# Split FFN weights kept in device memory by pass one and fetched by passes two and three; both variances ahead of the finishing steps

## The chip, the cores and the metric

The kernel runs on one core of a Trainium2 chip. The core has five engines that run their own instruction streams side by side and wait for each other through semaphores: TensorE (matmuls; PE in the profile, with its weight loads as PEld), VectorE (DVE), ScalarE (ACT), GpSimd (POOL) and SyncE (SP). Here SP does nothing but issue transfers; 16 DMA engines carry them between device memory and the core's on-chip memory. Matmul results land in PSUM, eight banks of 128 x 512 float32. The metric is the device time of one execution in microseconds; lower is better.

## What is computed

One layer of a streaming encoder over 2048 tokens of width 1024. First a token mixer (spatial gating) beside a cross-attention into 256 memory tokens, an output projection, a residual and a layer norm. Then a SwiGLU feed-forward network (FFN) of width 2816, a residual and a second layer norm. The change touches the FFN and its norms:

```python
def layer_norm(x, g, b):
    xf = x.astype(jnp.float32)
    mu = jnp.mean(xf, -1, keepdims=True)
    var = jnp.mean(jnp.square(xf - mu), -1, keepdims=True)
    y = (xf - mu) * lax.rsqrt(var + LN_EPS)
    return (y * g.astype(jnp.float32) + b.astype(jnp.float32)).astype(x.dtype)

def swiglu_ffn(x, w_in, w_down):
    h = x @ w_in
    return (jax.nn.silu(h[..., :D_FF]) * h[..., D_FF:]) @ w_down
...
        x = layer_norm(DEEPNORM_ALPHA * x + branch @ w_o[i], ln1_g[i], ln1_b[i])
        x = layer_norm(DEEPNORM_ALPHA * x + swiglu_ffn(x, ffn_w_in[i], ffn_w_down[i]), ln2_g[i], ln2_b[i])
```

## The kernel before

Everything is laid out feature-major: features on the 128 partitions, tokens along the free axis. Every operand of a matmul is split in two parts, `hi` (rounded to the float32r format) and `lo` (the rest), and a product is three matmuls: hi x hi, hi x lo, lo x hi (`PASSES`, L95). The splitting is `split` (L71): ScalarE casts (L73), VectorE subtracts (L74). Activations are split once; weights are split each time that they are loaded.

The mixer part handles the tokens in four chunks of 512 and ends near 752 us of the profile. It writes its normed output to a tensor `x1d` in device memory. The norm of its last chunk runs beside the FFN's start.

The FFN part goes over the tokens in three passes of 688, 680 and 680 tokens (`FPASSES`; here called passes 0, 1 and 2), and each pass goes over all the weights: 22 tiles of the FFN width in blocks of 5, 4, 4, 4 and 5 (`FBLOCKS`). A block has two parts.

- **Up** (`Pass.up`, L345), for each of the block's tiles: the gate and value columns of that tile together, by Strassen's scheme in Winograd's form, over halves of the model width and halves of the tokens. That is seven products of 4 x 3 = 12 matmuls each, every one with its own weight matrix of 128 x 512. `halves` (L97) loads the two weight tiles (r_u, 512 KB each) and makes four sums and differences of them (s_u, L109 to L113), on GpSimd for the first block of a pass and on VectorE for the others. `products` (L115) splits the seven matrices into tiles w, one behind the other, and runs the matmuls. Behind each product VectorE or ScalarE takes a stage (L354 to L368) that adds up the results and ends in silu(gate) x value, which is split into g.
- **Down** (`Pass.down`, L387), for each of the eight output feature tiles: the block's rows of the down projection come from device memory (r_d), are split into w_d (`weights`, L79; one tile for four rows, two tiles of two and three rows for five), and 3 matmuls per row and half of the tokens follow. VectorE adds the result to fa, which starts as the residual that `residual` (L380) loads from x1d (L406 for the first block, L409 for the others).

During the last down block of passes 0 and 1, `load` and `rest` (L319, L335) fetch and split the activations of the next pass. The layer norm of a pass (two `Norm`s, one for each half of its tokens, and one for the mixer's last chunk in pass 0) is taken in small steps between the products of the next pass's first block. `norm_steps` (L257) is a generator: `up` takes one step of it behind each product, 35 in the first block, and what is left is run at the block's end. A norm has these steps: the mean (a matmul with ones) and the centring (`centre`, L184; 4 steps), the variance and its inverse root (`var`, L220, on VectorE, ending in dg), and `finish` (L238; 4 steps), whose first act is a matmul that spreads dg over the partitions (`spread`). Finished tiles are stored to the output; the residual of the pass takes the same memory, so it loads behind those stores.

Three pools of on-chip tiles matter: `raw` (L68), four tiles of 4 KB per partition for anything loaded from device memory; `wsp` (L76), five tiles of 4 KB for split weights; and the eight PSUM banks, of which a tile's products use four. TensorE runs its instructions in the order in which the program emits them (`in_order`, L51). On the other engines, a scheduler chooses the order at build time by its own estimate; each engine then runs its stream strictly in that order. All loads and stores of the FFN part are issued by SP.

Of the kernel before, what the change touches and what calls it, by code (L numbers as in the profile page):

```python
# [17 lines left out]
P = 128  # L18
D = 1024
# [7 lines left out]
KD = D // P            # 8 contraction tiles of the model width  # L27
KB = (MIX + HEADS * HD) // P   # 10 contraction tiles of the branch width
NF = DFF // P          # 22 tiles of the FFN width
TC = 512               # tokens in a chunk of the mixer part  # L30
OPERANDS = (25, 3)             # operand tiles of the up projection that find room before and behind the mixer's end
NCHUNK = SEQ // TC
FPASSES = (688, 680, 680)      # tokens in a pass of the FFN part
# [6 lines left out]
def trunk_kernel(ctx, tc, xT, memT, wv, wuq, ws, bs, vg, vb, wmk, wmv, wo,  # L40
# [10 lines left out]
    def in_order(ins):  # L51
        """TensorE runs its instructions in the order in which they are emitted."""
        if last_on_pe:
            tc.add_manual_dep(ins.ins, last_on_pe.pop().name,
                              mybir.DependencyInfo(mybir.DependencyClass.NoSync, mybir.DependencyReason.DATA),
                              reason="order of TensorE")
        last_on_pe.append(ins.ins)
# [13 lines left out]
    def split(hi, lo, src, engine=nc.vector):  # L71
        """src = hi + lo exactly, each with the bits that one pass of TensorE carries."""
# [6 lines left out]
    def weights(src, shape, name, loads=1):  # L79
        """src [P, *shape], loaded at once and split; as shape[0] pairs [P, 2, shape[1]], several to a tile."""  # L80
        k, r, pairs = shape[0], raw([P, *shape], f"r_{name}"), []
        for i in range(loads):
            s = slice(i * k // loads, (i + 1) * k // loads)
            nc.sync.dma_start(out=r[:, s], in_=src[:, s])
        parts = -(-k * shape[1] // 512)
        for i in range(parts):
            s = slice(i * k // parts, (i + 1) * k // parts)
            n = s.stop - s.start
            w = wsp([P, 2, n, shape[1]], f"w_{name}_{i}")
            split(w[:, 0], w[:, 1], r[:, s])  # L90
# [6 lines left out]
    def halves(wa, wb, name, engine, in_place):  # L97
        """Two output tiles' weights, loaded: the left operands of the seven products in Strassen's scheme (in
        Winograd's form), over the two tiles x the halves of the contraction; by product."""
# [15 lines left out]
    def products(left, right, banks, name, stages, order, s4_after):  # L115
        """The seven products, into four banks; `stages` has the sums behind each of them."""
        q0, q1, q2, q3 = banks
        src, s4 = left
        out = {1: (q0, True, False), 2: (q0, False, True), 3: (q2, False, True), 4: (q3, False, True),
               5: (q2, True, False), 6: (q1, True, True), 7: (q3, True, False)}  # L120
        for n, p in enumerate(order):
            if n == s4_after:
                s4()
            to, start, stop = out[p]
            w = wsp([P, 2, 4, P], f"w{p}_{name}")
            split(w[:, 0], w[:, 1], src[p])
# [17 lines left out]
    def two_tiles(t, m, t0, n):  # L144
        """Feature tiles m and m + 1 of the tokens t0 to t0 + n."""
# [5 lines left out]
    class Norm:  # L151
        """Takes y feature tile by feature tile. Its sums over the tiles run on GpSimd; or, to end soon, on TensorE
        behind a VectorE that takes two tiles at a time (`pairs`)."""
# [24 lines left out]
        def variances(self, sq, start, stop):  # L178
            """One accumulation group for all columns: its start opens the whole bank."""
# [77 lines left out]
    def norm_steps(norms, stores, wait, pad):  # L257
        """The norms in small steps, to be taken between other work."""
# [10 lines left out]
        for _ in range(pad):  # L269
            yield  # L270
        for x, store in zip(norms, stores):
            x.var()
            for _ in range(5):
                yield
            yield from pairs(lambda a, b: x.finish(store, a, b))

    def inv_sqrt(r, v, t):
        """r = v ** -0.5 on VectorE: Newton steps from an estimate made of the bits, half the exponent; t is scratch."""
# [631 lines left out]
```

## Time and profile before

| | us |
|---|---|
| three runs | 2202.60, 2203.41, 2201.05 |
| their median | 2202.6 |
| span of the profiled execution, first to last instruction | 2205.3 |
| FFN part in that execution, first product to the end | 752.1 to 2205.3 |
| pass 0, pass 1, pass 2 begin at | 752.1, 1227.0, 1707.7 |

How to read the views that follow. The page gives busy time by engine; a busy TensorE is not yet one at its pace, since matmuls are pipelined. A row of the view of stretches has: from and to, the length, then for each engine its busy time and the number of its instructions, the TensorE clock that was granted (1.00 is full), the mean busy share of the DMA engines and the rate that they moved. Asked for one tile, such as h (the up projection's results in PSUM) or d (the down projection's), the row counts only the instructions that write or read that tile. A row of waits has: who waited, for whom, the total, the number of times and the longest. A row of groups has: line, engine, operation, out<-in and the count, then busy time and the mean duration in ns of one, then the idle time ahead of the group and what ended it. A row of the timeline has: start, length, engine, line, operation, and in brackets the idle time before it and what ended that. A row of transfers has: what was moved, the queue, the count, the size of one, and the median time from issue to landing.

### The profile page before, as it was taken

The page shows a single profiled execution, that of the slowest core. Times are in us where ns is not written, and L with a number is a line of the kernel's source. Part 1 is how long each engine was busy: PE and PEld are TensorE (multiplying, and loading weights), DVE is VectorE, ACT ScalarE, POOL GpSimd, SP SyncE. Part 2 cuts the span into 40 slices and gives each one's busy share as a digit, 9 for nine tenths or more (in the row PEclk, how much of TensorE's full clock was granted, in tenths as well). Part 3 has the DMA queues.
Part 4 walks back from the last instruction along what each step waited for, and adds up shares of the span by engine and source line. Part 5 has one row for each costly group of instructions (what it writes and reads, how often), then busy time and mean ns, then how long its engine had stood idle before and what let it go on. Part 6 is the DMA issues. An engine that isn't in the chain of part 4 may idle for free.

```text
span 2205.3 us, 34595 instructions
## 1 busy us (share of the span) xinstructions
PE 2120.0 (96%) x13130; PEld 2009.0 (91%) x13130; DVE 1704.4 (77%) x3014; ACT 970.7 (44%) x1886; POOL 397.3 (18%) x294
## 2 busy tenths in 40 slices
PE   9899999999999999999999889999999899999996
PEld 7888798798788889999999889999998899999996
DVE  7986796797788785776778986676689877677677
ACT  5553653654465452433434453343344534334344
POOL 1412321331322440000001820000004700000003
PEclk9999999999999999999999999999999999999998
DMA  6233324234334443212223242222224242221223
GB/s 211 77 110 123 112 78 158 92 96 149 117 96 133 139 132 92 87 58 86 87 68 91 89 160 88 82 68 82 82 66 119 83 153 67 87 86 58 89 75 99
DMA packets 88965, 221.93 MB, mean 101 GB/s; under 512 B 8416, under 2 KB 18656, under 8 KB 88800
## 3 DMA queue, kind: packets, MB, share of 16 engines
q1 hardware_dynamic: 88320, 218.66, 31.9%
q8 instruction: 103, 1.69, 0.3%
q0 software_dynamic: 480, 1.07, 0.2%
q14 instruction: 62, 0.51, 0.1%
HBM read 202.92 MB, written 16.78 MB: 100 GB/s over the span
## 4 chain that ended last, share of the span: by engine, by line
PE 66%; DVE 19%; DMA 5%; issue 4%; ACT 4%; POOL 2%; ACTq 0%; DVEq 0%; POOLq 0%; SPq 0%
PE h L60 36%; PE d L60 19%; PE v L60 5%; PE u L60 3%; DMA r_x<-in_xT 2%; DVE w L74 2%; DVE x L74 2%; DVE w_o L74 1%; DMA r_f<-x1d 1%; DVE w_u L74 1%; PE y L60 1%; POOL s_a L197 1%; ACT p L569 1%; DVE z L526 1%; DVE w_d L74 1%
## 5 line engine op out<-in xcount | busy, mean ns | idle before, releaser
L60 PE MATMUL h<-x,w 128*128 128x340 f32 (+1 forms) x5544 | 886.5, 322 | 14.7 <-DVE w L74 6.5
L60 PEld LDWEIGHTS h<-x,w 128*128 128x128 f32 x5544 | 875.1, 190 | 22.3 <-DVE w L74 8.9
L60 PE MATMUL d<-g,w_d 128*128 128x340 f32 (+3 forms) x3168 | 504.4, 320 | 7.5 <-DVE w_d L74 6.6
L60 PEld LDWEIGHTS d<-g,w_d 128*128 128x128 f32 x3168 | 497.4, 189 | 11.6 <-DVE w_d L74 8.3
L73 ACT CAST w<-s_u 128x512 fp32r<-128x512 f32 x264 | 163.4, 620 | 227.2 <-PE d L60 106.5
L74 DVE TENSOR_TENSOR w<-s_u,w 128x512 fp32r<-128x512 f32 x264 | 195.2, 741 | 46.1 <-ACT w L73 39.1
L60 PE MATMUL y<-br,w_o 128*128 128x512 f32 x960 | 224.4, 395 | 0.0
L60 PEld LDWEIGHTS y<-br,w_o 128*128 128x128 f32 x960 | 180.5, 188 | 42.0
L73 ACT CAST w<-r_u 128x512 fp32r<-128x512 f32 x198 | 122.3, 618 | 166.6 <-PE h L60 67.7
L60 PE MATMUL v<-w_v,x 128*128 128x512 f32 x768 | 188.4, 402 | 6.7 <-ACT w_v L73 5.0
L74 DVE TENSOR_TENSOR w<-r_u,w 128x512 fp32r<-128x512 f32 x198 | 150.0, 759 | 53.0 <-ACT w L73 49.7
L73 ACT CAST w_d<-r_d 128x512 fp32r<-128x512 f32 (+2 forms) x184 | 95.7, 521 | 206.6 <-PE d L60 151.3
L60 PEld LDWEIGHTS v<-w_v,x 128*128 128x128 f32 x768 | 144.1, 191 | 42.1 <-ACT w_v L73 5.0
L409 DVE TENSOR_TENSOR fa<-fa,d 128x340 f32<-128x340 f32 (+3 forms) x192 | 97.2, 506 | 100.3 <-PE d L60 100.3
L330 POOL TENSOR_TENSOR t<-r_f,r_f 128x340 f32<-128x340 f32 (+1 forms) x12 | 14.9, 1244 | 791.1 <-DMA r_f<-x1d 397.4
L74 DVE TENSOR_TENSOR w_d<-r_d,w_d 128x512 fp32r<-128x512 f32 (+2 forms) x184 | 110.5, 603 | 50.3 <-ACT w_d L73 47.1
L73 ACT CAST g<-c 128x340 fp32r<-128x340 f32 (+1 forms) x132 | 63.1, 478 | 93.9 <-DVE c L354 93.9
L60 PE MATMUL u<-xt,w_u 128*128 128x256 f32 x768 | 95.6, 280 | 0.0
L60 PEld LDWEIGHTS u<-xt,w_u 128*128 128x128 f32 x768 | 92.7, 188 | 0.0
L60 PE MATMUL u<-x,w_u 128*128 128x256 f32 x576 | 78.6, 288 | 11.3 <-DVE u L535 6.9
L60 PEld LDWEIGHTS u<-x,w_u 128*128 128x128 f32 x576 | 72.1, 191 | 13.9 <-issue 6.6
L74 DVE TENSOR_TENSOR w_o<-r_o,w_o 128x512 fp32r<-128x512 f32 (+1 forms) x96 | 67.8, 716 | 21.1 <-ACT w_o L73 20.8
(185 smaller groups left out, 2537.6 us busy)
## 6 DMA issues: line engine op xcount, KB each, us to landing
r_u<-in_w SPq DMA_DIRECT2D x132, 512.0 KB, 3.4
r_d<-in_w SPq DMA_DIRECT2D x72, 256.0 KB, 2.7
r_d<-in_w SPq DMA_DIRECT2D x56, 320.0 KB, 2.9
r_u<-in_wuq SPq DMA_DIRECT2D x32, 512.0 KB, 3.6
r_o<-in_wo SPq DMA_DIRECT2D x32, 512.0 KB, 3.6
r_v<-in_wv SPq DMA_DIRECT2D x31, 512.0 KB, 4.4
y<-in_xT SPq DMA_DIRECT2D x16, 512.0 KB, 5.8
x1d<-y SPq DMA_DIRECT2D x16, 512.0 KB, 4.0
```

Of the source, the lines that this page charges most:

```text
L60: in_order(nc.tensor.matmul(*args, **kw))
L73: nc.scalar.copy(hi, src)
L74: engine.tensor_sub(lo, src, hi.bitcast(F32))
L197: nc.gpsimd.tensor_add(self.s2, self.s2, sq)
L330: nc.gpsimd.tensor_sub(t3, b22, b12)
L409: nc.vector.tensor_add(y, y, p)
L526: nc.vector.tensor_scalar(z[h][:, b], z[h][:, b], mv[:, b, 0:1], rs[:, b:b + 1], ALU.subtract, ALU.mult)
L569: nc.scalar.activation(pr[:, h, :], svs[h // 2][:, h % 2, :], AF.Exp, scale=HD ** -0.5, bias=mxv[:, h:h + 1], accum_out=sm[:, h:h + 1])
```

## The change

The first pass splits the weights as before, and then stores each split tile (hi and lo together) to a tensor of its own in device memory. The store is issued from ScalarE's queue (`keep`). Passes 1 and 2 make no weight sums and no splits: they fetch the kept tiles (`ready`), by SP, in turn into a tile of `wsp` and into a tile of `raw`, and the matmuls read those directly. This holds for the up projection's 154 matrices and the down projection's 56 tiles. A fetched tile of the up projection has 512 KB; the two raw tiles that stood for seven matrices had 1 MB together.

In `norm_steps` the order of a seam's steps changes. Before, each norm had its variance, five steps of other work, and its four finishing steps, one norm behind the other. Now both variances come first, with four steps behind each, then four more steps, and then the finishing steps of both. The norms of passes 0 and 1 start after 6 steps instead of 4.

```diff
+    kept = {}
+
+    def keep(key, w):
+        t = dram.tile(list(w.shape), F32, tag=key, name=f"k_{key}")
+        nc.scalar.dma_start(out=t, in_=w.bitcast(F32))
+        kept[key] = t
+
+    turns = []
+
+    def ready(key, name):
+        src = kept[key]
+        turns.append(key)
+        if len(turns) % 2:
+            w = wsp(list(src.shape), f"w_{name}")
+            nc.sync.dma_start(out=w.bitcast(F32), in_=src)
+            return w
+        r = raw(list(src.shape), f"r_{name}")
+        nc.sync.dma_start(out=r, in_=src)
+        return r.bitcast(F32R)
...
     def weights(...):
+        have = key is not None and f"{key}_0" in kept
+        if not have:
+            r = raw([P, *shape], f"r_{name}")
...
+            if have:
+                w = ready(f"{key}_{i}", f"{name}_{i}")
+            else:
+                w = wsp([P, 2, n, shape[1]], f"w_{name}_{i}")
+                split(w[:, 0], w[:, 1], r[:, s])
+                if key is not None:
+                    keep(f"{key}_{i}", w)
...
     def products(...):
-            w = wsp([P, 2, 4, P], f"w{p}_{name}")
-            split(w[:, 0], w[:, 1], src[p])
+            if src:
+                w = wsp([P, 2, 4, P], f"w{p}_{name}")
+                split(w[:, 0], w[:, 1], src[p])
+                if key is not None:
+                    keep(f"{key}_{p}", w)
+            else:
+                w = ready(f"{key}_{p}", f"{p}_{name}")
...
     def norm_steps(norms, stores, wait, pad):
...
+        for x in norms:
+            x.var()
+            for _ in range(4):
+                yield
+        for _ in range(4):
+            yield
         for x, store in zip(norms, stores):
-            x.var()
-            for _ in range(5):
-                yield
             yield from pairs(lambda a, b: x.finish(store, a, b))
...
-            products(halves(w1[f], w1[NF + f], f"u{name}", sums, False), lambda p, k, b: self.x[p][k][:, b], banks,
-                     name, {p: then(stage) for p, stage in stages.items()}, (1, 6, 2, 5, 7, 3, 4), 0)
+            left = None if no else halves(w1[f], w1[NF + f], f"u{name}", sums, False)
+            products(left, lambda p, k, b: self.x[p][k][:, b], banks,
+                     name, {p: then(stage) for p, stage in stages.items()}, (1, 6, 2, 5, 7, 3, 4), 0, key=f"u{f}")
...
-                return weights(w2[m, :, f0:f0 + nb, :], [nb, P], f"d{no}_{blk}_{m}_{ci}")
+                return weights(w2[m, :, f0:f0 + nb, :], [nb, P], f"d{no}_{blk}_{m}_{ci}", key=f"d{blk}_{m}")
...
-                work = norm_steps(norms, [pa.store(0, h), pa.store(h, n)], 4, 0)
+                work = norm_steps(norms, [pa.store(0, h), pa.store(h, n)], 6, 0)
```

More of the change, by code (lines that the diff above doesn't have):

```diff
@@ L77, in wsp, with weights @@
         return common.tile(shape, F32R, tag="wsp", bufs=5, name=name)
[L79 to L84, printed above, removed]
-        parts = -(-k * shape[1] // 512)
-        for i in range(parts):
-            s = slice(i * k // parts, (i + 1) * k // parts)
-            n = s.stop - s.start
-            w = wsp([P, 2, n, shape[1]], f"w_{name}_{i}")
-            split(w[:, 0], w[:, 1], r[:, s])
+    kept = {}
[14 more added lines that the diff above has]
+        return r.bitcast(F32R)
+    def weights(src, shape, name, loads=1, key=None):
+        k, pairs = shape[0], []
+        parts = -(-k * shape[1] // 512)
+        cuts = [slice(i * k // parts, (i + 1) * k // parts) for i in range(parts)]
+        have = key is not None and f"{key}_0" in kept
+        if not have:
+            r = raw([P, *shape], f"r_{name}")
+            for i in range(loads):
+                s = slice(i * k // loads, (i + 1) * k // loads)
+                nc.sync.dma_start(out=r[:, s], in_=src[:, s])
+        for i, s in enumerate(cuts):
+            n = s.stop - s.start
+            if have:
[5 more added lines that the diff above has]
+                    keep(f"{key}_{i}", w)
             pairs += [w[:, :, j, :] for j in range(n)]
@@ L113, in halves, with products @@
         return {1: a11, 2: a12, 3: s4, 4: a22, 5: s1, 6: s2, 7: s3}, lambda: engine.tensor_sub(s4, a12, s2)
-    def products(left, right, banks, name, stages, order, s4_after):
+    def products(left, right, banks, name, stages, order, s4_after, key=None):
         q0, q1, q2, q3 = banks
-        src, s4 = left
+        src, s4 = left or (None, None)
         out = {1: (q0, True, False), 2: (q0, False, True), 3: (q2, False, True), 4: (q3, False, True),
@@ L121, in products @@
         for n, p in enumerate(order):
-            if n == s4_after:
+            if src and n == s4_after:
                 s4()
             to, start, stop = out[p]
-            w = wsp([P, 2, 4, P], f"w{p}_{name}")
-            split(w[:, 0], w[:, 1], src[p])
+            if src:
[5 more added lines that the diff above has]
+                w = ready(f"{key}_{p}", f"{p}_{name}")
             for k in range(4):
```

## The prediction

> **What bounds the kernel now.** First the page: which engine is busy.
>
> ```profile
> span 2205.3 us, 34595 instructions
> ...
> PE 2120.0 (96%) x13130; PEld 2009.0 (91%) x13130; DVE 1704.4 (77%) x3014; ACT 970.7 (44%) x1886; POOL 397.3 (18%) x294
> ```
>
> TensorE is busy 96% of the span, so most of the kernel can't get shorter by taking work off other engines. The question is where TensorE runs below its pace. So, second, the view of stretches, cut at the FFN's blocks, for the up projection's matmuls alone (columns: length, busy time and count on TensorE, weight loads, VectorE, ScalarE, then granted clock, DMA share, GB/s).
>
> ```profile
> 752.10:833.20 81.10, 71.95 (x420) 68.70 (x419) 12.22 (x24) 4.44 (x10) 0.96 0.39 121
> ...
> 1120.00:1186.10 66.10, 66.08 (x420) 65.95 (x420) 12.33 (x24) 4.51 (x10) 1.00 0.21 66
> 1227.00:1313.50 86.50, 71.55 (x420) 68.18 (x420) 12.09 (x24) 4.45 (x10) 0.94 0.31 98
> ...
> 1597.60:1663.00 65.40, 65.39 (x420) 65.32 (x420) 12.22 (x24) 4.47 (x10) 1.00 0.23 67
> 1707.70:1790.50 82.80, 70.90 (x420) 67.74 (x420) 12.12 (x24) 4.45 (x10) 0.94 0.32 97
> ```
>
> Each row is one block of 5 tiles x 7 products x 12 = 420 matmuls. Undisturbed it takes 66.1 us in pass 0 (344 columns) and 65.4 us in passes 1 and 2 (340 columns), with TensorE busy throughout. The first block of each pass takes 81.1, 86.5 and 82.8 us: **15.0, 21.1 and 17.4 us are lost at the three seams**. The same view for the down projection's blocks of 240 matmuls (TensorE, weight loads, VectorE):
>
> ```profile
> 833.20:870.90 37.70, 37.70 (x240) 37.58 (x240) 7.69 (x15) 1.00 0.32 93
> 1186.10:1227.00 40.90, 38.53 (x240) 37.55 (x240) 6.52 (x13) 1.00 0.46 144
> 1313.50:1350.90 37.40, 37.40 (x240) 37.24 (x240) 7.62 (x15) 1.00 0.44 151
> 1663.00:1707.70 44.70, 39.90 (x240) 38.73 (x240) 7.45 (x15) 0.96 0.47 131
> ```
>
> The last block of pass 0 loses 3.2 us and that of pass 1 7.3 us. Who is late? All work in the same stretches, with VectorE third, ScalarE fourth and GpSimd fifth:
>
> ```profile
> 1227.00:1313.50 86.50, 74.25 (x447) 71.25 (x446) 77.68 (x140) 46.40 (x94) 50.55 (x37) 0.94 0.31 98
> ...
> 1597.60:1663.00 65.40, 65.40 (x422) 65.40 (x421) 51.04 (x92) 30.58 (x61) 0.83 (x1) 1.00 0.23 67
> 1663.00:1707.70 44.70, 39.94 (x242) 38.82 (x241) 43.88 (x75) 18.86 (x44) 20.17 (x18) 0.96 0.47 131
> ```
>
> At a seam VectorE has 77.7 us of work for a block that TensorE could do in 65.4, and in the last down block it is busy 43.9 of 44.7 us: VectorE is the bound there. In the middle it has 51.0 of 65.4 and binds nothing. TensorE's waits in the two seam blocks, then in the last down block of pass 1, say the same:
>
> ```profile
> PE rstd_b L60 <- DVE dg_b L230: 6.0, 1, 6.0
> PE mean_b L60 <- POOL s_b L176: 2.9, 1, 2.9
> PE h L60 <- DVE w L74: 1.6, 2, 1.4
> ```
> ```profile
> PE rstd_b L60 <- DVE dg_b L230: 6.3, 1, 6.3
> ```
> ```profile
> PE d L60 <- DVE w_d L74: 4.4, 2, 3.3
> ```
>
> **The change part by part.** (1) Passes 1 and 2 lose every split and every weight sum. In the first block of pass 1 these are:
>
> ```profile
> L74 DVE TENSOR_TENSOR w<-s_u,w 128x512 fp32r<-128x512 f32 x20 | 18.0, 907 | 3.0 <-ACT w L73 3.0
> ...
> L74 DVE TENSOR_TENSOR w<-r_u,w 128x512 fp32r<-128x512 f32 x14 | 13.2, 947 | 0.2 <-ACT w L73 0.2
> ```
>
> 31.2 us leave VectorE, and 77.7 - 31.2 = 46.5 us remain for 65.4: it stops being the bound. GpSimd loses its sums too. What is late next is TensorE itself: 65.4 us plus the norms' own matmuls, which are the 74.25 - 71.55 = 2.7 us between two rows above, so 68.1 us. That is a gain of at most 18.4 us (86.5 - 68.1) and 14.7 us (82.8 - 68.1). I take 16 and 13, leaving 2 us each for weights that arrive late; the bounds are 8 and 7 (rival C) and the full amounts. In the last down block of pass 1 the subtractions of w_d go, 8 of each of
>
> ```profile
> L74 DVE TENSOR_TENSOR w_d<-r_d,w_d 128x384 fp32r<-128x384 f32 x56 | 35.5, 634 | 20.2 <-ACT w_d L73 19.5
> ...
> L74 DVE TENSOR_TENSOR w_d<-r_d,w_d 128x256 fp32r<-128x256 f32 x56 | 25.6, 457 | 8.8 <-ACT w_d L73 8.8
> ```
>
> or 8.7 us: 35.2 us remain for 37.4. That barely fits, and the next pass's operands still hold raw tiles, so I take 4 of the 7.3 us (bounds 0 and 7.3). All other blocks of passes 1 and 2 gain nothing: TensorE is already full.
>
> (2) Pass 0 gains 210 stores on ScalarE's queue, each behind VectorE's subtraction. Steady state of pass 0, ScalarE then VectorE:
>
> ```profile
> 1001.34 0.62 ACT L73 CAST w_d<-r_d 128x512 fp32r<-128x512 f32 x1 [0.88 <-PE h L60]
> 1003.23 0.62 ACT L73 CAST w_d<-r_d 128x512 fp32r<-128x512 f32 x1 [1.26 <-PE h L60]
> ```
> ```profile
> 1002.00 0.69 DVE L74 TENSOR_TENSOR w_d<-r_d,w_d 128x512 fp32r<-128x512 f32 x1
> ```
>
> The subtraction ends at 2.69; ScalarE's next cast starts at 3.23, because it waits for TensorE to free a tile. An issue on ScalarE is not in this trace; SP's nearest takes 0.37 us:
>
> ```profile
> L668 SPq DMA_DIRECT2D x1d<-y x16: 359/366/382, 263.1 to 813.6; - x16
> ```
>
> It fits the gap of 0.54 us, so in the steady state it costs nothing. Queued behind the waiting store are the next cast, the copies and SiLUs, and for those VectorE waits. In the first block VectorE is behind, and cast, subtraction (0.91) and issue in turn are 0.62 + 0.91 + 0.37 = 1.9 us of the 81.1 / 35 = 2.3 us per product. That leaves little: I take a loss of 5 us, between 0 (enough gaps) and 15 (a wait of 0.4 us on each of 35). In the last down block of pass 0, where VectorE is as full, I take 3 (0 to 8).
>
> A split tile (5 of them) is now held until its store has landed: 0.62 + 0.69 + 0.37 + 4.0 = 5.7 us of the 5 x 1.89 = 9.4 us between uses, so the hold is hidden while stores land within 7.7 us.
>
> (3) Transfers. A tile of the up projection in pass 0 takes 66.1 / 5 = 13.2 us and now moves 7 stores and 2 loads of 512 KB, 4.72 MB: 357 GB/s. In passes 1 and 2 it is 512 KB per 65.4 / 35 = 1.87 us: 281 GB/s. The densest seven microseconds of the trace, and landings:
>
> ```profile
> 821.00:828.00 7.00, 7.00 (x47) 7.00 (x45) 4.20 (x9) 3.09 (x8) 0.00 (x0) 1.00 1.02 400
> ```
> ```profile
> r_u<-in_w SPq DMA_DIRECT2D x132, 512.0 KB, 3.4
> ...
> x1d<-y SPq DMA_DIRECT2D x16, 512.0 KB, 4.0
> ```
>
> 400 GB/s, with TensorE full beside it. So pass 0 would run its DMA engines at 89%; I take 2 us of delay, between 0 and the 43 of rival B. In passes 1 and 2 a load has 8 products (four raw tiles, used every second time) or 15 us to land in 3.4: hidden; without that cover it is rival C.
>
> (4) The norms' steps. From the variance to the matmul that spreads it there are now 12 steps (one per product, 22 us at pace) for 5 (9 us). The chain took longer than 9:
>
> ```profile
> 1259.75 0.70 PE L60 MATMUL var_b<-ones,s_b 128*86 128x1 f32 x8
> ...
> 1275.94 1.52 PE L60 MATMUL rstd_b<-dg_b,ones 86*128 86x344 f32 x2 [6.04 <-DVE dg_b L230]
> ```
>
> 16.2 us, on a crowded VectorE, so the 6 us wait goes; it is inside the gains of (1). The first mean comes 2 steps later (3.7 us), more than its wait of 2.9. The finish ends at step 34 of 35 instead of 30, so output stores and the residual loads behind them on SP come some 7.5 us later. Cover: the first down block's results can wait in PSUM for several feature tiles. If that cover fails it costs about 3 us per seam. In pass 0 the one norm's finish moves 3 steps (5.7 us) later under the same cover.
>
> **Sum:** gains 16 + 13 + 4 = 33; losses 5 + 3 + 2 = 10; net -23 us. The profiled execution (span 2205.3) stands 2.7 us above the median of the three runs, 2202.6 (2201.05 to 2203.41). 2205.3 - 23 = 2182 as a span, 2202.6 - 23 = **2180 us** as a time.
>
> **The rivals.**
> *B, slower: the stores saturate the DMA engines in pass 0.* The page's average is less kind than the burst:
>
> ```profile
> q1 hardware_dynamic: 88320, 218.66, 31.9%
> ```
>
> 218.66 MB in 31.9% of 2205.3 us is 311 GB/s. At that ceiling 4.72 MB take 15.2 us per tile against 13.2, and 22 tiles lose 43 us; seams at 25 instead of 33 and the other losses of 8 make it +26: 2229 us. It turns slower when 22 tiles lose over 25 us, below about 330 GB/s. Against it: the 400 of the burst; for it: the burst was loads only. The Trainium skill, page "DMA: Bandwidth & Descriptors", section "Where 436 GB/s comes from", lets about 358 GB/s bind between HBM and SBUF, which would put pass 0 exactly at the limit. The measured 400 speaks against that for a core alone. Chance 0.14.
> *C: the weights come late at the seams.* SP issues in order, and its weight loads stand behind 16 output stores, 4 residual loads and, in the last down block, 8 operand loads that hold raw tiles. If the 15 us of look-ahead are used up, half of the 33 go: 2202.6 - 16.5 + 10 = 2196 us. For it: a block at 281 GB/s plus 5.6 MB of outputs and residuals in 68 us is 350 GB/s. Against it: stores and loads hang on the same products, so they seldom drift apart by 10 us. Chance 0.18.
> *D: nothing is lost in pass 0 and the seams clear fully:* 18.4 + 14.7 + 7.3 = 40, 2162 us. Chance 0.12. The forecast has 0.56, its own range being 2168 to 2192.
>
> **How the numbers follow.** The range 2162 to 2203 takes in the forecast, C and D and leaves out B. A measurement of this kernel tells about 0.2% (4.4 us) from no change. Faster: 0.56 + 0.12 + two thirds of C = 0.80; same: the rest of C, 0.06; slower: B, 0.14.
>
> **What would show it.** First up blocks of passes 1 and 2 at 68 to 71 us with no wait for dg_b; last down block of pass 1 near 40; blocks in the middle unchanged at 65.4; pass 0's middle up blocks at 66.1 per 420 matmuls with TensorE waiting for no cast (if they are longer and its waits name w tiles behind stores, B). Wrong if TensorE waits for fetched weights at the seams (C), or if pass 0's first block grows by over 15 us.

## The result and the profile after

The changed kernel takes 2229.82 us (median of 4 runs, 2228.78 to 2230.57), the kernel before 2202.45 us in the same session (4 runs, 2201.05 to 2203.41). The ratio is 1.0126, 95% interval 1.0112 to 1.0141: **1.3% slower**, where 1% faster was forecast.

The page of the changed kernel, first the engines, then the transfers of the largest queue:

```profile
span 2227.9 us, 34054 instructions
...
PE 2129.0 (96%) x13130; PEld 2011.4 (90%) x13130; DVE 1315.4 (59%) x2442; ACT 733.8 (33%) x1450; POOL 324.1 (15%) x254
...
q1 hardware_dynamic: 125760, 359.71, 48.9%
```

VectorE has lost 389 us of work (1704.4 to 1315.4) and ScalarE 237, and yet the span has grown by 22.6 us. The view of stretches for the up projection's matmuls, cut at the blocks, tells where: the first, second middle and last up block of pass 0, then first and last of pass 1 and the first of pass 2.

```profile
752.00:849.50 97.50, 77.65 (x420) 71.99 (x419) 12.31 (x24) 4.46 (x10) 0.89 0.77 279
979.30:1037.90 58.60, 54.49 (x336) 52.63 (x336) 9.81 (x19) 3.61 (x8) 1.00 0.72 262
1160.90:1239.10 78.20, 70.30 (x420) 67.22 (x420) 12.39 (x24) 4.52 (x10) 0.98 0.69 250
1283.00:1356.90 73.90, 69.44 (x420) 67.16 (x420) 12.27 (x24) 4.46 (x10) 0.98 0.86 298
1641.10:1706.50 65.40, 65.40 (x420) 65.28 (x420) 12.29 (x24) 4.49 (x10) 1.00 0.78 253
1745.10:1815.30 70.20, 67.84 (x420) 65.54 (x420) 12.27 (x24) 4.45 (x10) 1.00 0.86 296
```

Beside it the middle up block of pass 0 in the kernel before, which the prediction did not show (4 tiles, 336 matmuls):

```profile
953.90:1006.80 52.90, 52.84 (x336) 52.77 (x336) 9.76 (x19) 3.62 (x8) 1.00 0.23 66
```

A block's time is read from its first matmul to the first matmul of the next block; the stretch is that time rounded to 0.1. The sums:

| stretch | before, us | after, us | difference |
|---|---|---|---|
| pass 0: first up block | 81.1 | 97.5 | +16.4 |
| pass 0: first down block | 37.7 | 39.5 | +1.7 |
| pass 0: three middle up blocks | 158.6 | 175.3 | +16.7 |
| pass 0: three middle down blocks | 90.6 | 96.6 | +6.0 |
| pass 0: last up block | 66.1 | 78.2 | +12.1 |
| pass 0: last down block | 40.9 | 43.9 | +3.0 |
| pass 1: first up block | 86.5 | 73.9 | -12.6 |
| pass 1: last down block | 44.7 | 38.6 | -6.1 |
| pass 2: first up block | 82.8 | 70.2 | -12.6 |

The seams give 31.3 us, and 2.2 us more come from the last down block of pass 2. But pass 0, which goes from 752 to 1227 before and to 1283 after, costs **56 us**, and it costs them in every one of its blocks, the steady ones too.

Who is waited for there? TensorE's waits between 752 and 1240 us:

```profile
PE h L60 <- DVE w L74: 19.8, 20, 1.7
PE h L60 <- ACT w L73: 15.9, 9, 6.7
PE d L60 <- DVE w_d L74: 6.6, 4, 1.7
PE h L60 <- ACT m L405: 1.5, 1, 1.5
```

In the kernel before, TensorE waited for no w tile in any up block of pass 0 but the first. Now the split weights come late all through the pass, mostly by 1 to 2 us at a time, although VectorE is busy for 36.4 and ScalarE for 22.1 of the 58.6 us of a middle block (all work in it, VectorE third, ScalarE fourth):

```profile
979.30:1037.90 58.60, 54.52 (x339) 52.72 (x337) 36.41 (x66) 22.06 (x44) 0.00 (x0) 1.00 0.72 262
```

Engines with that much idle time that still deliver late stand behind something in their own streams. The waits of ScalarE and VectorE in the middle block 979.3 to 1037.9 name it:

```profile
ACT c L398 <- DVE c L397: 17.2, 4, 5.8
ACT m L406 <- PE h L60: 9.0, 4, 3.5
```

And the timeline at one of these places:

```profile
1002.18 0.52 DVE L407 TENSOR_TENSOR c<-h,u 128x344 f32<-128x344 f32 x1 [0.46 <-PE h L60]
1004.06 0.52 DVE L397 TENSOR_TENSOR c<-h,u 128x344 f32<-128x344 f32 x1 [1.36 <-PE h L60]
1004.61 0.49 ACT L398 ACTIVATE c<-c 128x344 f32<-128x344 f32 x1 [5.75 <-DVE c L397]
1005.00 0.61 ACT L73 CAST w<-r_u 128x512 fp32r<-128x512 f32 x1
...
1005.64 0.69 DVE L74 TENSOR_TENSOR w<-r_u,w 128x512 fp32r<-128x512 f32 x1
...
1006.39 1.72 PEld L60 LDWEIGHTS h<-x,w 128*128 128x128 f32 x11 [0.43 <-DVE w L74]
```

Read it upwards. TensorE waits for a subtraction, that waits for its cast, and the cast stands in ScalarE's stream behind the SiLU (L398), which has waited 5.75 us for a sum of VectorE, which waited for TensorE. In the kernel before, the casts of the next tile's first four products stood *ahead* of that SiLU (there L359), and it waited for nothing. ScalarE alone, in the kernel before:

```profile
973.42 0.61 ACT L73 CAST w<-r_u 128x512 fp32r<-128x512 f32 x1
974.91 0.62 ACT L73 CAST w<-s_u 128x512 fp32r<-128x512 f32 x1 [0.88 <-PE h L60]
976.80 0.62 ACT L73 CAST w<-r_u 128x512 fp32r<-128x512 f32 x1 [1.27 <-PE h L60]
978.74 0.62 ACT L73 CAST w<-s_u 128x512 fp32r<-128x512 f32 x1 [1.31 <-PE h L60]
979.26 0.49 ACT L359 ACTIVATE c<-c 128x344 f32<-128x344 f32 x1
```

The built streams of pass 0 tell it for each tile: the number of the next tile's casts that stand ahead of a tile's SiLU is 4 throughout in the kernel before, and 2, 1, 0, 1 (first block), then 3, 2, 1 or 3, 0, 1 in the changed kernel. A reader of the diff doesn't see that: the order of all but TensorE's stream is chosen when the program is built.

### The profile page after: what moved, and what is told of

It reads as the page before. It is cut to its first block, busy times and chain, and to the rows that moved or that the text cites. A ratio compares the mean times of both kernels' runs of the same rounds, so it can differ in the third digit from the quotient of the medians.

```text
span 2227.9 us, 34054 instructions
## 1 busy us (share of the span) xinstructions
PE 2129.0 (96%) x13130; PEld 2011.4 (90%) x13130; DVE 1315.4 (59%) x2442; ACT 733.8 (33%) x1450; POOL 324.1 (15%) x254
## 4 chain that ended last, share of the span: by engine, by line
PE 69%; DVE 14%; DMA 6%; ACT 4%; issue 4%; POOL 2%; ACTq 0%; SPq 0%; DVEq 0%; POOLq 0%
PE h L60 37%; PE d L60 21%; PE v L60 5%; PE u L60 3%; DMA r_x<-in_xT 2%; DVE w_o L74 2%; DMA r_f<-x1d 1%; DVE w L74 1%; DVE w_u L74 1%; POOL s_a L233 1%; DMA r_o<-in_wo 1%; ACT p L609 1%; DVE z L566 1%; DVE x L74 1%; DVE s L519 1%
## 5 line engine op out<-in xcount | busy, mean ns | idle before, releaser
L60 PE MATMUL h<-x,w 128*128 128x344 f32 (+1 forms) x3696 | 626.2, 324 | 41.6 <-DVE w L74 19.8
L60 PEld LDWEIGHTS h<-x,w 128*128 128x128 f32 x3696 | 591.7, 191 | 55.4 <-DVE w L74 30.3
L60 PE MATMUL d<-g,w_d 128*128 128x344 f32 (+3 forms) x2112 | 350.7, 321 | 10.0 <-DVE w_d L74 8.0
L60 PEld LDWEIGHTS d<-g,w_d 128*128 128x128 f32 x2112 | 335.1, 189 | 13.2 <-DVE w_d L74 10.0
L60 PE MATMUL h<-x,r 128*128 128x340 f32 x1848 | 315.9, 320 | 0.9 <-DMA r<-k_u 0.9
L60 PEld LDWEIGHTS h<-x,r 128*128 128x128 f32 x1848 | 293.5, 189 | 2.8 <-DMA r<-k_u 1.2
L60 PE MATMUL d<-g,r_d 128*128 128x340 f32 (+2 forms) x1056 | 179.2, 318 | 1.0 <-DMA r_d<-k_d 1.0
L60 PEld LDWEIGHTS d<-g,r_d 128*128 128x128 f32 x1056 | 166.8, 188 | 2.1 <-DMA r_d<-k_d 1.3
L398 ACT ACTIVATE c<-c 128x340 f32<-128x340 f32 (+1 forms) x66 | 32.3, 490 | 320.9 <-DVE c L397 320.8
L406 DVE TENSOR_TENSOR u<-h,u 128x340 f32<-128x340 f32 (+1 forms) x66 | 33.9, 513 | 165.8 <-PE h L60 165.5
```

The source lines that it names most:

```text
L60: in_order(nc.tensor.matmul(*args, **kw))
L398: nc.scalar.activation(c12, c12, AF.Silu)
L406: 2: lambda: nc.scalar.activation(m1, q0, AF.Silu), 5: lambda: nc.vector.tensor_add(u4, q2, u2),
```

## The experiments

Three theories stood against each other at first. **Traffic:** the stores take the DMA engines or the tiles (rival B of the prediction). **Place:** the stores on ScalarE's queue make ScalarE and VectorE late; this divides into the *issue itself* (a store waits for VectorE's subtraction, and all behind it waits too) and the *order* in which the build then puts the two streams. **Hold:** a split tile isn't free until its store has landed. Where a single run is given, the number in brackets is the kernel before beside it. The kernel before took 2201.05 to 2208.52 us in all these sessions, so a few us between two whole times tell nothing. A middle up block of pass 0 that waits for nothing takes 52.8 to 52.9 us in whichever run, so the argument goes by blocks.

### Who issues the stores: the traffic alone loses nothing

`e3_store_sp`, the changed kernel with one word changed:

```diff
-        nc.scalar.dma_start(out=t, in_=w.bitcast(F32))
+        nc.sync.dma_start(out=t, in_=w.bitcast(F32))
```

> The changed kernel with its stores issued by SP instead of ScalarE. Theory queue (ScalarE stands behind its stores, which stand behind VectorE): pass 0 falls from 531 us to 475 to 490, its middle up blocks from 58.4 to 53 or 54. Theory hold (a split tile that stays taken until its store has landed leaves too few tiles, and the casts are put later in ScalarE's stream): pass 0 stays above 510 and the middle up blocks above 56. Theory DMA: no change at all.

2186.63 us [2204.95]: 43 us below the changed kernel and faster than before. Its second middle up block:

```profile
970.70:1023.50 52.80, 52.80 (x336) 52.67 (x335) 9.78 (x19) 3.62 (x8) 1.00 0.82 309
```

The block is at TensorE's pace while 309 GB/s move, more than the 262 at which the changed kernel lost 5.7 us. All stores, all bytes and the hold of the tiles are still there, so traffic and hold fall as causes by themselves. The counter-check, `e2_traffic`, puts extra stores of the finished g tiles on SP into pass 0 of the kernel before (they go to tensors that nobody reads):

```diff
+            if no == 0:
+                for i in range(5):
+                    t = dram.tile([P, 2, self.n], F32, tag=f"x{f}_{i}", name=f"x{f}_{i}")
+                    nc.sync.dma_start(out=t, in_=g.bitcast(F32))
```

> The kernel before, and in pass 0 each finished tile g is stored five times to device memory from SP's queue: about 3.5 MB per tile of the up projection, as many bytes as the changed kernel's seven stores, but no split tile is held by them and ScalarE issues none. These stores are extra; the output is that of the reference. Theory DMA (the engines are saturated): the middle up blocks of pass 0 grow from 52.9 us to the 58.4 of the changed kernel. Theories hold and queue: they stay within 1 us of 52.9, and pass 0 at 475 to 480 us.

```profile
982.60:1035.40 52.80, 52.80 (x336) 52.70 (x336) 9.77 (x19) 3.62 (x8) 1.00 0.67 247
```

The middle is unchanged. The whole is slower, 2241.94 us [2204.95], for another reason: SP issues in order, and the weight loads of the first down block stand behind these stores. At the end of the first up block, which takes 106.4 us, TensorE waits 23.6 us for the first w_d.

### The hold and the distance of the store: little

`e4_six_tiles` gives every sixth split tile a place of its own (`sq` gives one tile up for it), `e5_lag` emits each store behind the next split instead of its own, and `e9_four_tiles` is the kernel before with one split tile less.

```diff
# e4_six_tiles
+            if len(used) % 6 >= 5:
+                return open_pools["wspx"].tile(shape, F32R, tag="wspx", name=name)
...
-    pool("sq", 4, "right")
+    pool("sq", 3, "right")
+    pool("wspx", 1, "right")
# e5_lag
-        nc.scalar.dma_start(out=t, in_=w.bitcast(F32))
+        late_stores.append((t, w))
+        if len(late_stores) > 1:
+            flush()
...
# e9_four_tiles
-        return common.tile(shape, F32R, tag="wsp", bufs=5, name=name)
+        return common.tile(shape, F32R, tag="wsp", bufs=4, name=name)
```

> The changed kernel with six tiles for split weights in the FFN part instead of five (and three tiles instead of four for the norms' squares, to make room). Theory hold: the middle up blocks of pass 0 fall from 58.4 us by at least 2, towards 54, and pass 0 from 531 by 15 to 35. Theory queue: under 1 us in the blocks and 5 in the pass. Theory DMA: no change.

> The changed kernel, stores still on ScalarE's queue, but each is emitted one split tile later, so that VectorE's subtraction is done when ScalarE comes to it. Theory wait (ScalarE stands at each store until VectorE has subtracted): pass 0 falls from 531 us to 480 to 500, its middle up blocks from 58.4 to under 54. Theory place (the stores' mere presence in ScalarE's stream changes where the casts are put; a cast that is placed behind a stage waits for TensorE): pass 0 stays above 510 and the blocks above 56.

> The kernel before with four tiles for split weights instead of five, in all its parts. ScalarE's stream then has three casts of the next tile's weights ahead of each SiLU of the second gate half, where the kernel before has four and the changed kernel three, one or none. Theory place: three casts (5.6 us of TensorE work) cover the SiLU's wait; the middle up blocks of pass 0 stay within 1 us of 52.9. If one tile less already costs what the changed kernel lost, they grow to over 56.

The middle blocks of e4 take 56.9 us (whole 2221.97 [2204.95]), those of e5 56.7 to 56.9 (whole 2212.46 [2208.31]), against 58.2 to 58.6 in the changed kernel: each gives back 1.3 to 1.9 us of the 5.3 to 5.7. Neither is a clean test, since the build orders the streams anew here too: the casts ahead of the SiLU in these blocks are 4, 3, 1 or 4, 1, 1 in e4 and 3, 1, 0 in e5. For e5 this is what "place" expected, above 56 us. In e9 the blocks stay at 52.8; with three casts ahead of every SiLU nothing is lost. (Its whole is slower, 2217.39 [2203.49], of which the mixer part, with a tile less, takes 7.4 us.) So it isn't the number of tiles.

### Stores that the build doesn't mind: nothing is lost

`e6_tiny` is the kernel before with a store of 32 bytes per partition, on ScalarE's queue, behind each split of an up matrix in pass 0: the same 154 issues, each with the same wait for VectorE's subtraction.

```diff
             split(w[:, 0], w[:, 1], src[p])
+            if name.startswith("0_"):
+                t = dram.tile([P, 8], F32, tag=f"t{p}_{name}", name=f"t{p}_{name}")
+                nc.scalar.dma_start(out=t, in_=w[:, 1, 3, P - 8:P].bitcast(F32))
```

> The kernel before, and behind each split of the up projection in pass 0 ScalarE issues a store of 32 bytes per partition of that tile, 4 KB instead of 512 KB. These stores are extra; the output is that of the reference. Passes 1 and 2 split as before. If ScalarE's queue is the cause, with hardly any bytes moved, pass 0's middle up blocks grow from 52.9 us to 57 to 59 and the first from 81 to 95 to 100. If the bytes or the long hold of a tile are needed too, the middle blocks stay under 54.

```profile
959.10:1011.90 52.80, 52.80 (x336) 52.68 (x335) 9.77 (x19) 3.61 (x8) 1.00 0.26 68
```

Nothing is lost in the middle; the whole takes 2211.05 us [2208.31], and what is lost is in the first block, 86.8 us for 81.1. That was a miss for the theory of the issue in the steady state. And it gave the lead: with tiny stores the casts and stages of the middle blocks stand in ScalarE's stream in the very order of the kernel before. With 512 KB stores they don't.

### The order of ScalarE's stream alone: part of it, and a riddle

A dependency that carries no wait, of each instruction on the one named before it, holds a stream in a given order. `e12_order_only` is the kernel before, with no store at all, its casts and stages of pass 0 on ScalarE held in the changed kernel's order. `e10_forced` is the reverse: the changed kernel, stores on ScalarE, with ScalarE's casts and stages in the order of e3.

```diff
+    chain = [acts[k] for k in ACT_ORDER.split()]
+    for a, b in zip(chain, chain[1:]):
+        tc.add_manual_dep(b.ins, a.ins.name,
+                          mybir.DependencyInfo(mybir.DependencyClass.NoSync, mybir.DependencyReason.DATA),
+                          reason="order of ScalarE")
```

> The kernel before, without any store or fetch, with the casts and stages of pass 0's blocks on ScalarE held in the changed kernel's order. Theory place: the middle up blocks of pass 0 grow from 52.9 us to 56 to 59 and pass 0 from 475 to over 505, with no byte more moved. Theory hold (the tiles themselves are taken too long) or DMA: they stay at 52.9.

> The changed kernel, stores still on ScalarE's queue, with the casts and stages of pass 0's blocks on ScalarE held in the order of the kernel with stores on SP (four casts ahead of a SiLU); the stores fall where the scheduler puts them between these. Theory place: the middle up blocks of pass 0 fall from 58.4 us to 53 to 54.5 and the total by 20 or more. Theory wait: the stores still stand behind VectorE and the blocks stay above 56.

```profile
962.70:1017.70 55.00, 53.65 (x336) 52.59 (x336) 9.75 (x19) 3.62 (x8) 1.00 0.16 49
```
```profile
976.40:1034.50 58.10, 55.11 (x336) 54.13 (x336) 9.77 (x19) 3.58 (x8) 0.97 0.74 268
```

The rows are the second middle up block of each. e12 (first row, 2226.49 us [2203.49]) loses 1.7 to 2.1 us per middle block, about a third of the 5.3 to 5.7, without a single store; 56 to 59 us were expected, and 54.6 to 55.0 came. But e10 (second row, 2219.36 [2203.49]) loses all of it still, 58.1 to 58.7 us where 53 to 54.5 were expected, in a new guise: the wait is now for ScalarE's copy of the first product.

```profile
PE h L94 <- ACT m L443: 14.7, 13, 2.1
```

Taken alone these two would acquit the order. What they leave out is VectorE: the order of its built stream has changed as well, in the changed kernel and in e10. There subtractions of the next tile stand behind three stages that wait for TensorE's products, with no subtraction between these; the kernel before alternates the two.

### Both streams: all that the middle blocks lose

`e14_both_bad` is the kernel before, no store, with the casts, subtractions, weight sums and stages of pass 0 on **both** engines in the changed kernel's order. `e13_both_good` is the changed kernel with both streams in the order of e6, stores included. `e15_sp_order` is the changed kernel with both streams in the order of e3; its stores stand on ScalarE's queue where the build puts them.

```diff
+    for to, order in ((acts, ACT_ORDER), (dves, DVE_ORDER)):
+        chain = [to[k] for k in order.split()]
...
```

> The kernel before, without any store, but in pass 0 ScalarE's and VectorE's streams of the FFN stand in the order that the changed kernel has. If the order of the two streams is all that the loss consists of, the middle up blocks of pass 0 take 57.5 to 58.6 us as in the changed kernel, with no store in the program. If only ScalarE's order counts, 54.5 to 55.0 us as in the run that set ScalarE's alone. If the stores count as well, something between 55 and 57.5 us.

> The changed kernel, stores of 512 KB on ScalarE's queue as in the change, but in pass 0 the casts, subtractions, sums and stages of the FFN on ScalarE and on VectorE stand in the order that the kernel before (with its tiny stores) has, the stores each beside its cast. The run that set ScalarE's casts and stages alone left VectorE's stream reordered. If the order of the two streams is all that the loss consists of, the middle up blocks of pass 0 take 52.8 to 53.2 us, and the first up block 88 to 95 us. If a store of 512 KB in ScalarE's stream costs by itself, they stay at 56 to 58.6 us with this order too. A part of each: 54 to 56 us.

> The changed kernel, its 512 KB stores still on ScalarE's queue, but in pass 0 the casts, subtractions, weight sums and stages on ScalarE and on VectorE stand in the order that the version with SP's stores has (its VectorE takes a tile's weight sums later than the kernel before does, when the slower loads of r_u have landed); the stores stand where the build puts them in that order. If the two orders are the whole cause, the middle up blocks take 52.8 to 53.3 us with ScalarE issuing every store, and the whole 2180 to 2195 us. If a store on ScalarE's queue costs by itself, they stay at 55 us or more and the whole above 2205 us.

The same view for the second middle up block of e14, e13 and e15:

```profile
974.30:1032.90 58.60, 54.47 (x336) 52.62 (x336) 9.81 (x19) 3.62 (x8) 1.00 0.15 46
```
```profile
988.10:1042.80 54.70, 53.34 (x336) 52.71 (x336) 9.74 (x19) 3.61 (x8) 1.00 0.84 302
```
```profile
975.20:1028.10 52.90, 52.88 (x336) 52.74 (x336) 9.79 (x19) 3.62 (x8) 1.00 0.88 317
```

e14 is the changed kernel's middle block to a tenth of a microsecond, 58.6 with 54.47 busy (58.6 with 54.49), with no store in the program and 46 GB/s instead of 262. Even its longest wait is the same one, at another line number:

```profile
ACT c L447 <- DVE c L446: 18.3, 4, 5.8
```

The whole takes 2259.28 us [2206.59]. All of pass 0 takes 523.5 us in e14 (753.4 to 1276.9) against 474.9 before: the order alone costs 48.6 us, where the changed kernel loses 56.1. (Not in quite the same blocks: e14's three middle down blocks take 3 us more than the changed kernel's, its first up block takes 6.4 us less and its last down block 4.1 us less.) e15 closes it from the other side: the same 512 KB stores on the same queue of ScalarE, both streams in a good order, and the middle blocks are at the pace, 52.85, 52.84 and 52.85 us; the whole takes 2197.38 us, 32 less than the changed kernel (2180 to 2195 were expected; its first up block and its last down block, below, are longer than e3's).

e13 missed what was expected of it: its middle up blocks take 57.9, 54.7 and 58.3 us instead of 52.8 to 53.2, its first up block 110.4 instead of 88 to 95, and the whole 2218.14 [2206.59]. For the middle, its rows say why. VectorE, from 880 to 1240 us:

```profile
DVE s_u L243 <- DMA r_u<-in_w: 33.3, 16, 4.0
```

The order of the kernel before takes a tile's first weight sum early, in the midst of the stages. There the loads of r_u had landed (the median was 3.4 us). With the stores beside them they take 5.1:

```profile
r_u<-in_w SPq DMA_DIRECT2D x44, 512.0 KB, 5.1
```

VectorE stands still for that sum, up to 4.0 us, with stages behind it; TensorE's waits there are for such a stage (c, 9.7 us in 9 waits), no longer for a subtraction. In the kernel before VectorE waits 1.1 us for r_u in its middle and last blocks. The order of e3 takes the sums later; in e15 the loads land no sooner (6.1 us), and VectorE waits 8.6 us for them at no cost to the middle blocks. So traffic isn't wholly innocent: an order that fits the quiet memory doesn't fit the busy one.

| order of the streams of pass 0 | stores | second middle up block, us |
|---|---|---|
| kernel before's | none | 52.8 |
| kernel before's | tiny, ScalarE (e6) | 52.8 |
| changed kernel's on ScalarE, VectorE's free | none (e12) | 55.0 |
| changed kernel's on both | none (e14) | 58.5 |
| changed kernel's on both | 512 KB, ScalarE (the change) | 58.6 |
| e3's on ScalarE, VectorE's free | 512 KB, ScalarE (e10) | 58.1 |
| kernel before's on both | 512 KB, ScalarE (e13) | 54.7 |
| e3's on both | 512 KB, ScalarE (e15) | 52.8 |
| e3's | 512 KB, SP (e3) | 52.8 |

### The seams: which part of the change clears them

`e1_old_steps` is the changed kernel with the old order of the norms' steps.

```diff
-        for x in norms:
+        for x, store in zip(norms, stores):
             x.var()
-            for _ in range(4):
+            for _ in range(5):
                 yield
...
-                work = norm_steps(norms, [pa.store(0, h), pa.store(h, n)], 6, 0)
+                work = norm_steps(norms, [pa.store(0, h), pa.store(h, n)], 4, 0)
```

> The changed kernel with the seam's steps in the old order (variance, five steps, finish, one norm behind the other; start after 4 steps). In the changed kernel the first up blocks of passes 1 and 2 take 73.9 and 70.2 us. If the freed VectorE alone cleared the seams, they stay within 2 us of that. If the new order of the steps did it, the waits for dg_b come back and each block grows by about 6 us, to 80 and 76. Pass 0 (531 us from its first product to that of pass 1) stays as it is, within 5 us.

2230.35 us [2204.95], the same as with the new order. The first up blocks of passes 1 and 2 take 73.1 and 69.7 us (73.9 and 70.2 in the changed kernel); the down blocks after them are longer, 38.1 for 37.4 and 39.1 for 37.3. The one wait for dg_b that is left in each is that at the kernel's end, 4.8 us; before there were three, 17.2 us in all. What the fetched weights free, VectorE above all, but ScalarE and GpSimd too, clears the seams with either order.

### The first block, and a version that beats both

In the first block of pass 0 the stores on SP help less (e3: 94.2 us against 97.5, and 81.1 before). At the end of that block TensorE waits 10.9 us for the weights of the first down block, whose loads stand at SP behind four residual loads. `e8_early` takes e3 and issues the residual behind the first two weight fetches of the down block; `e7_store_pool` is the changed kernel with the stores on GpSimd's queue; `e11_pool_loads` is e8 with the first down block's weights loaded by GpSimd.

```diff
# e8_early, upon e3_store_sp
+                if blk == n == 0:
+                    self.residual()
...
-                pa.residual()
# e11_pool_loads, upon e8_early
-                nc.sync.dma_start(out=r[:, s], in_=src[:, s])
+                queue.dma_start(out=r[:, s], in_=src[:, s])
...
+                               queue=nc.gpsimd if no == blk == 0 else nc.sync)
# e7_store_pool
-        nc.scalar.dma_start(out=t, in_=w.bitcast(F32))
+        nc.gpsimd.dma_start(out=t, in_=w.bitcast(F32))
```

> The changed kernel with its stores issued by GpSimd, which has nothing to do in the middle of pass 0. The middle up blocks of pass 0 should be 52.9 us as with SP. In the first block GpSimd has the weight sums, which now stand behind stores that wait for VectorE: 85 to 100 us against 81.1 before. SP's loads are free, so the 10.9 us wait of the down projection for its first weights, seen with stores on SP, goes. Total 2175 to 2190.

> The changed kernel with stores on SP, and the residual loads of a pass emitted behind the fetch of the first down block's first two weight tiles instead of ahead of it. If the 10.9 us wait for w_d came from the residual loads, the first up block of pass 0 falls from 94.2 us to 84 to 88 and the total from 2186.6 to about 2178; if the stores ahead of them on SP are what delays the weights, under 4 us are won.

> Stores on SP, residual loads behind the first weights (as in the run e8_early), and the eight loads of the first down block's weights in pass 0 issued by GpSimd, so that they don't stand behind SP's stores. The waits for w_d of 7.2 us in that block go: first down block of pass 0 from 45.4 to 38 to 41 us, total from 2181.8 to 2174 to 2180.

| | first up | first down | second middle up | last up | last down | whole, us |
|---|---|---|---|---|---|---|
| before | 81.1 | 37.7 | 52.8 | 66.1 | 40.9 | 2202.45 |
| the change | 97.5 | 39.5 | 58.6 | 78.2 | 43.9 | 2229.82 |
| e7 | 97.0 | 39.7 | 53.9 | 68.8 | 46.8 | 2207.73 [2208.31] |
| e15 | 101.1 | 39.6 | 52.8 | 67.2 | 46.9 | 2197.38 [2203.49] |
| e3 | 94.2 | 39.8 | 52.8 | 67.0 | 42.0 | 2186.63 [2204.95] |
| e8 | 86.3 | 45.4 | 52.8 | 67.5 | 40.4 | 2181.84 [2208.31] |
| e11 | 84.5 | 37.9 | 52.8 | 67.4 | 41.6 | 2173.38 [2203.49] |

The residual ahead of the weights costs 7.9 us of the first up block; moved, it leaves the first down block's weights late (45.4), and another queue for these brings that back to 37.9. e7 missed: 2175 to 2190 us and middle blocks of 52.9 were expected, and it takes 2207.73 us, as long as the kernel before, with middle up blocks of 57.1, 53.9 and 54.0. Its two streams stand there in the order of the kernel before, as in e13, and VectorE waits for the landing of r_u as there:

```profile
DVE s_u L139 <- DMA r_u<-in_w: 24.1, 13, 3.5
```

So a queue that computes nothing in these blocks wasn't enough by itself. Nor do stores on ScalarE do as well as on SP where the engines are crowded: e15 has the FFN's streams of e3 in pass 0 and still takes 11.5 us more there (503.9 against 492.5), 7.0 of them in the first up block and 4.9 in the last down block; the order of the norms' steps, which that run leaves to the build, differs there too, and the two weren't told apart. e11 is the best version: 2173.38 us (4 runs, 2169.55 to 2176.04), ratio to the kernel before 0.9852, interval 0.983 to 0.9873. It keeps the whole change and loses 5.7 us in pass 0 (480.6 against 474.9).

## Why the prediction was wrong

**Right: part (1), the seams.** Forecast 16 + 13 + 4 = 33 us; measured 12.6 + 12.6 + 6.1, and 2.2 that weren't forecast, together 33.5. That the totals agree so well is in part luck: the first up block of pass 1 gave 3.4 us less than forecast, and the last down blocks of passes 1 and 2 made up for it. VectorE has this much in the first up block of pass 1, where 46.5 of 65.4 were foretold:

```profile
1283.00:1356.90 73.90, 70.87 (x444) 69.81 (x445) 43.65 (x107) 26.97 (x56) 16.87 (x18) 0.98 0.86 298
```

The block still takes 73.9 us, not 68 to 71, partly because weights come late: rival C in small.

```profile
PE h L60 <- DMA w<-k_u: 3.0, 1, 3.0
```

In e3, e7, e8, e11 and e15 the same block takes 69.0 to 69.1. The middle of passes 1 and 2 stayed at 65.4 as forecast.

**Wrong: part (2), pass 0.** The step that failed is "It fits the gap of 0.54 us, so in the steady state it costs nothing". The arithmetic holds: an issue on ScalarE took 0.33 us, and in e6 (154 issues in the pass) and e15 (210) they cost nothing in the steady state. The issues of the changed kernel's up projection:

```profile
L83 ACTq DMA_DIRECT2D k_u<-w x154: 326/327/2424, 746.7 to 1237.4; - x154
```

What failed is the assumption beneath it: that the stores are put into the streams *as they stood in the trace of before*. They were built anew, in another order, on ScalarE and on VectorE, and that order costs 5.3 to 5.7 us in each middle up block, 2 in each middle down block and 12.1 in the last up block, where 0 was forecast. For the first block 5 us (0 to 15) were forecast and 16.4 came, though the term as it was meant, issues of ScalarE that wait for VectorE, is about right: the tiny stores of e6 cost 5.7 us there. For the last down block 3 (0 to 8) were forecast and 3.0 came; with the order alone (e14) that block takes 39.8 us, less than before, so these 3.0 aren't the order's. The prediction did name what is queued behind a waiting store (the next cast, the copies and SiLUs, and VectorE behind them). It priced it by one gap beside one cast, of w_d at that, and took no account of how many casts run ahead of the SiLU, which is the slack that the new order spends.

In the first block there is more. e14, with the order alone, takes 91.2 us there, 10 of the 16.4 us; the norm's squares stand in ScalarE's stream too, and in the changed kernel TensorE waited 6.66 us for a cast that stands behind five of them (L229), three of which wait for GpSimd's sums. The last of them, the cast, and TensorE:

```profile
777.28 0.63 ACT L229 ACTIVATE sq_a<-y 128x512 f32<-128x512 f32 x1 [0.71 <-POOL s_a L233]
777.81 0.60 ACT L73 CAST w<-r_u 128x512 fp32r<-128x512 f32 x1
...
778.47 11.75 PE L60 MATMUL h<-x,w 128*128 128x344 f32 x62 [6.66 <-ACT w L73]
```

How the rest divides between these squares, the issues, the residual on SP and the landing of r_u wasn't told apart; e15 and e13, which set the FFN's order but not the norm's, have 101.1 and 110.4 us there. The cause is shown for the middle and last up blocks; for the first block it is open in part.

**Right: part (3), transfers,** and the refusal of rival B's mechanism. B said 2229 us, and 2229.8 came: a coincidence. B needs transfers that stay below about 330 GB/s; in e15's first middle up block, with all the stores, 339 GB/s moved and TensorE was at its pace, and e14 has the loss at 46.

```profile
892.20:945.00 52.80, 52.80 (x336) 52.70 (x336) 9.79 (x19) 3.62 (x8) 1.00 0.93 339
```

The sign that the prediction gave for B, longer middle blocks with TensorE waiting for w tiles, did appear: a late w tile doesn't tell slow stores from a changed order. The Trainium skill, page "DMA: Bandwidth & Descriptors", section "Where 436 GB/s comes from", lets about 358 GB/s bind between HBM and SBUF. This case went above it: e11 moved 371 GB/s over 50 us (822 to 872), with TensorE busy for 49.79 of them, and the changed kernel 420 GB/s over 7 us (1144.5 to 1151.5). Rival C's 16 output stores at a seam are 8 in the trace of the kernel before; its 5.6 MB are right. The hold of a split tile, "hidden" in the forecast, is hidden in the middle blocks (e3, e15). What the prediction missed here is the landing of r_u, 3.4 us before, 5.8 in the changed kernel, which made the old order itself unfit (e13, e7).

**Not borne out: part (4), the norms' steps.** The wait for dg_b went, as forecast, but not because of them: it went in e1 too.

**The chances.** All rivals with a loss took it from the DMA engines or from late fetches. That the build would answer the change with another order of the streams was no case at all, though the description of the kernel says that all engines but TensorE run in an order that the build chooses.

What stays open: why the build orders the streams so for 512 KB stores on ScalarE and not for tiny ones or for SP's. The runs show that it does, and what the order costs, not how it chooses. Open too is whether the new order of the norms' steps would have cleared the wait for dg_b without the freed VectorE.

## What to carry to other kernels

Where a scheduler orders an engine's stream at build time, a new instruction in that stream can move all the others: after any change compare the built streams of all engines, above all how many producers of the next tile stand ahead of the first instruction that waits for the bottleneck. Stores issued from a queue that computes nothing were the best choice here when that queue was SP's (e3), and not when it was GpSimd's (e7): judge a queue by the streams that the build then makes, or hold these by hand. When an order is suspected, set the order of every engine that takes part and test it from both sides, the bad order without the suspected work and the work in a good order; one engine alone gave about 2 of 5.7 us in one direction and nothing in the other.

## What was not expected of the hardware

TensorE kept its full pace, busy for all of 52.80 us at a granted clock of 1.00, while 339 GB/s of loads and stores moved beside it (e15, 892.2 to 945.0). A store's issue took 0.33 us on ScalarE and 0.32 on SP (e3). The granted clock was below 1.00 in first blocks, where TensorE idled: 0.89 in the changed kernel's, where the 420 matmuls were busy 77.65 of 97.5 us, against 0.96 and 71.95 of 81.1 before. But it didn't go by the idle time alone: in e3's first block they were busy 70.95 of 94.2 us at 0.95. What sets it wasn't tried.
